# Stored split weights a step later, kept weight pieces two a step, and another order of PSUM pools in a two-layer trunk

## The chip, the cores and the metric

One core of a Trainium2 chip. The metric is the device time of one execution in microseconds (us), as the median of three runs. On the core work TensorE (PE in the profile; PEld is its weight load), VectorE (DVE), ScalarE (ACT), GpSimd (POOL) and SyncE (SP), which here only issues transfers (DMA).

## The reference

A trunk of two layers over 2048 frames of 1024 channels, all in float32:

```python
# layer A
h = rms_norm(x, a_norm);  u, z = split(h @ a_w_in)               # 1024 -> 2 x 1024
pooled = trailing_means(u, windows 2/4/8/16 by channel group) - u
x = x + ((grouped(pooled @ a_w_group) * a_scale) * silu(z)) @ a_w_out
x = x + (p[0] @ ple_w[0]) * sigmoid(x @ ple_gate_w[0])
# once, shared by layer B
k, v = split(rms_norm(x, kv_norm) @ w_kv);  k = rms_norm per head
# layer B
q, z = split(rms_norm(x, b_norm) @ b_w_in);  q = rms_norm per head
o = stick_breaking_attention(q, k, v)    # 16 heads of 64; A[t,s] = beta[t,s] * prod_{s<j<t}(1 - beta[t,j])
x = x + (o * silu(z)) @ b_w_out
x = x + (p[1] @ ple_w[1]) * sigmoid(x @ ple_gate_w[1])
```

## The kernel before

Every dense product is made of three TensorE passes. [...] A split takes one ScalarE instruction (copy, or a scaling by a norm's gain) and one subtract on VectorE or GpSimd. The split pair is twice as large as its source.

**First stage.** Four passes s = 0 to 3, one for each 512 frames. A pass has 22 steps (`STEPS`): 0 to 7 are `run_u` and `run_z` in turn for the four channel groups (some with a small group product, `run_m`), 8 to 11 `run_o` (output weights of layer A), 12 to 15 `run_g` (gate and per-layer embedding), 16 and 17 queries, 18 and 19 keys, 20 and 21 values (`run_kvq`). A step of 512 or 256 output channels has 48, 60 or 96 matmuls of 512 columns. The main loop (L541) first calls the load of the next step's weights (`load_w`), and then runs this step.

`load_w` (L94) loads units of 256 KB into `wraw` (3 buffers), splits each (L110 and L112, or with a gain L116 and L117) into `wpair` (12 buffers of 512 KB). The input weights of layer A (`wi`) are wanted in all four passes. In pass 0 each of their 32 split units is stored to DRAM (L121); passes 1 to 3 load them from there already split (L105).

Layer B's weights for z, output, gate and embedding are also split once, during the first stage, in 56 pieces (`keep`, L508): a raw load into pool `io` (L510), the split into a tile of tag `t4` (3 buffers; L178 and L179, or L517 and L518), a store to `wzd`, `wod`, `wgd` or `wld` (L520). The list `kept` is emptied by the main loop: in a pass before the last, one piece after each of the steps 8 to 21 and a second one after steps 8 and 12; in the last pass, one after each of the steps 8 to 15.

**Order of the work.** The kernel's text gives each instruction a place in program order. A scheduler in the compiler then makes each engine's own queue: it takes program order as the priority and fills in what it finds ready, by its own estimate of times. A buffer that is used again brings the waits with it. Some instructions are pinned behind their predecessor on the engine (`keep_in_program_order`). Once made, each engine's queue, SyncE's with the transfers included, runs strictly in its order.

**PSUM in the first stage.** Eight banks of 128 x 512: six for dense sums (`psd`), taken in turn, and two for transposes (`pst`). A value step (`token_major`, kind "v") reads its sums with ScalarE (L399), sends rows to the next partition by transfers issued from ScalarE (L403 to L410), and stores differences of values later (L416 to L420).

**Second stage.** Attention by 512 queries, heads and 512 keys. `front` makes logits (L607, L608, on the diagonal L610) in pool `psl`, then sigmoid (L613) and a running product (L615). `turn` transposes into `psa` (L626) and splits (L629, L630), `gather` sums values into `pso` (L638, L639). Between them, a generator `beside` gives pieces of dense work in `psd2`: `gate_z` for z (L667 to L671 in `piecewise`, weights loaded by L678 from `wzd`) and `post` for what comes behind attention. Four pools of two banks each are opened in the order `psl`, `psa`, `pso`, `psd2`, so they hold banks 0-1, 2-3, 4-5 and 6-7. A pool's first tile waits until the readers of what had stood in the pool's banks are done; SBUF pools of the second stage stand likewise on the first stage's.

Of the kernel before, what the change touches and what calls it, by code (L numbers as in the profile page):

```python
# [22 lines left out]
NSUB = S // W5  # L23
# [3 lines left out]
STEPS = 22  # L27
# [3 lines left out]
def f(ap):  # L31
    return ap.bitcast(F32)
# [3 lines left out]
def trunk_kernel(ctx, tc, x, p, a_norm, a_w_in, a_w_group, a_scale, a_w_out, kv_norm, w_kv,  # L36
                 k_norm, b_norm, b_w_in, b_q_norm, b_w_out, ple_w, ple_gate_w, out):
    nc = tc.nc
# [51 lines left out]

    state = {"w": 0, "first": True}
    split_once = {}

    def load_w(pools, src, kts, c0, n, gain=None, kept=None):  # L94


        wraw, wpair = pools
        units = []
        srcr = src.rearrange("(k q) n -> q k n", q=P)
        kk = min(W5 // n, kts)  # L100
        for k0 in range(0, kts, kk):
            pr = wpair.tile([P, 2, kk, n], F32R, tag="wpair", name="wpair")
            units.append(pr)
            if (kept, c0, k0) in split_once:
                nc.sync.dma_start(out=f(pr), in_=split_once[kept, c0, k0])  # L105
                continue
            raw = wraw.tile([P, kk, n], F32, tag="wraw", name="wraw")
            (nc.scalar if state["first"] else nc.sync).dma_start(out=raw, in_=srcr[:, k0 : k0 + kk, c0 : c0 + n])
            if gain is None:
                A.copy(out=pr[:, 0], in_=raw)  # L110
                state["w"] += 1
                (G if state["w"] % 3 else V).tensor_tensor(out=pr[:, 1], in0=raw, in1=f(pr[:, 0]), op=ALU.subtract)  # L112
            else:
                for j in range(kk):
                    g = gain[:, k0 + j : k0 + j + 1]
                    A.activation(out=pr[:, 0, j], in_=raw[:, j], func=AF.Identity, scale=g)  # L116
                    V.scalar_tensor_tensor(out=pr[:, 1, j], in0=raw[:, j], scalar=g, in1=f(pr[:, 0, j]),  # L117
                                           op0=ALU.mult, op1=ALU.subtract)
            if kept is not None:
                d = split_once[kept, c0, k0] = dram.tile([P, 2, kk, n], F32, name=f"{kept}_{c0}_{k0}")  # L120
                nc.sync.dma_start(out=d, in_=f(pr))  # L121
        return units

    def wst(units, kt, hl, c0, n=P):
# [19 lines left out]
    with ExitStack() as st:  # L144
# [32 lines left out]
        def split(pr, src, lo):  # L177
            A.copy(out=pr[:, 0], in_=src)  # L178
            lo.tensor_tensor(out=pr[:, 1], in0=src, in1=f(pr[:, 0]), op=ALU.subtract)  # L179
# [170 lines left out]
        def settle():  # L350
            while late:
                late.pop(0)()
# [108 lines left out]
        def turn_rows(dst, rows):  # L461
            n = rows.shape[0]
            pt = turned()
            T.transpose(pt[:, 0, :n], rows, ident[:n, :n])
            A.copy(out=dst, in_=pt[:, 0, :n])

        def load_gains(vs, dst):

            rows = t2.tile([len(vs) * KT, P], F32, tag="grow", name="grow", bufs=1)
            for i, v in enumerate(vs):  # L470
                nc.sync.dma_start(out=rows[i * KT : (i + 1) * KT], in_=v.rearrange("(k q) -> k q", q=P))
            turn_rows(dst, rows)

        def load_head_gains():
            rows = t2.tile([2, P], F32, tag="hrow", name="hrow", bufs=1)
            for i, v in enumerate((k_norm, b_q_norm[0])):
                for e in range(2):
                    nc.sync.dma_start(out=rows[i : i + 1, e * HD : (e + 1) * HD], in_=v.rearrange("(o d) -> o d", o=1))
            gs = t2.tile([P, 2], F32, tag="gs", name="gs", bufs=1)
            turn_rows(gs, rows)  # L480
            V.scalar_tensor_tensor(out=gqk, in0=gs[:, 1:2], scalar=HD ** -0.5, in1=gs[:, 0:1],
                                   op0=ALU.mult, op1=ALU.mult)

        steps = []
        for s in range(NSUB):
            for g in (3, 2, 1, 0):
                def load(g=g, z=0):
                    w = (load_w(wp, a_w_in[0], KT, z * D + g * 256, 256, g_a, "wi"),)
                    if z and g == 0:
                        w += (load_w(wp, a_w_group[0, 0], 2, 0, 256),)  # L490
                    if not z and g < 3:
                        w += (load_w(wp, a_w_group[0, g + 1], 2, 0, 256),)
                    return w
                steps.append((load, lambda *w, s=s, g=g: run_u(s, g, *w)))
                steps.append((lambda load=load: load(z=1), lambda *w, s=s, g=g: run_z(s, g, *w)))
            for b in range(4):
                steps.append((lambda b=b: (load_w(wp, a_w_out[0], KT, b * 256, 256),),
                              lambda *w, s=s, b=b: run_o(s, b, *w)))
            for b in range(4):
                steps.append((lambda b=b: (load_w(wp, ple_gate_w[0], KT, b * 256, 256),  # L500
                                           load_w(wp, ple_w[0], 2, b * 256, 256)),
                              lambda *w, s=s, b=b: run_g(s, b, *w)))
            for kind, wsrc, base, gain in (("q", b_w_in[0], 0, g_b), ("k", w_kv, 0, g_kv), ("v", w_kv, D, g_kv)):
                for b in range(2):
                    def load(wsrc=wsrc, base=base, b=b, gain=gain, s=s, kind=kind):
                        return (load_w(wp, wsrc, KT, base + b * W5, W5, gain),)
                    steps.append((load, lambda *w, s=s, kind=kind, b=b: run_kvq(s, kind, b, *w)))
        def keep(src, kts, k0, o, dst, gain=None):  # L508
            raw = io.tile([P, kts, P], F32, tag="io", name="kraw")
            nc.sync.dma_start(out=raw, in_=src.rearrange("(k q) n -> q k n", q=P)[:, k0 : k0 + kts, o * P : (o + 1) * P])  # L510
            pr = t2.tile([P, 2, kts, P], F32R, tag="t4", name="kpair", bufs=3)
            if gain is None:
                split(pr, raw, G)
            else:
                for j in range(kts):
                    g = gain[:, k0 + j : k0 + j + 1]
                    A.activation(out=pr[:, 0, j], in_=raw[:, j], func=AF.Identity, scale=g)  # L517
                    V.scalar_tensor_tensor(out=pr[:, 1, j], in0=raw[:, j], scalar=g, in1=f(pr[:, 0, j]),  # L518
                                           op0=ALU.mult, op1=ALU.subtract)
            nc.sync.dma_start(out=dst, in_=f(pr))  # L520

        kept = []
        for o in range(KT):
            for i in range(2):
                kept.append(lambda o=o, i=i: keep(b_w_in[0], 4, 4 * i, 8 + o, wzd[o][:, i], g_b))
                kept.append(lambda o=o, i=i: keep(b_w_out[0], 4, 4 * i, o, wod[o][:, i]))
                kept.append(lambda o=o, i=i: keep(ple_gate_w[1], 4, 4 * i, o, wgd[o][:, i]))
            kept.append(lambda o=o: keep(ple_w[1], 2, 0, o, wld[o]))
# [9 lines left out]
            pass  # L538
        load_gains([a_scale[0], b_norm[0], kv_norm], gains)
        load_head_gains()  # L540
        for i, (_, run) in enumerate(steps):  # L541
            after = steps[i + 1][0]() if i + 1 < len(steps) else None
            run(*ready)
            ready = after
            step, s = i % STEPS, i // STEPS
            if step >= 8 and (s + 1 < NSUB or step < 16):
                kept.pop(0)()
                if s + 1 < NSUB and step in (8, 12):
                    kept.pop(0)()
        assert not kept  # L550
        settle()


    with ExitStack() as st:
        wpair = st.enter_context(tc.tile_pool(name="wpair2", bufs=6))
        t2 = st.enter_context(tc.tile_pool(name="s2", bufs=2))
        kap = st.enter_context(tc.tile_pool(name="kap", bufs=1))
        psl = st.enter_context(tc.tile_pool(name="psl", bufs=2, space=bass.MemoryType.PSUM))
        psa = st.enter_context(tc.tile_pool(name="psa", bufs=2, space=bass.MemoryType.PSUM))
        pso = st.enter_context(tc.tile_pool(name="pso", bufs=2, space=bass.MemoryType.PSUM))  # L560
        psd = st.enter_context(tc.tile_pool(name="psd2", bufs=2, space=bass.MemoryType.PSUM))

        NK = 4
# [248 lines left out]
        for n in range(4 * len(slots) + LAG_G):  # L812
            i, j = divmod(n, 4)
# [60 lines left out]
```

## Time and profile before

| | us |
|---|---|
| median of 3 runs (lowest to highest) | 2873.58 (2870.37 to 2878.38) |
| the profiled execution's own time | 2875.26 |
| its span, first to last instruction | 2873.5 |
| TensorE busy | 2782.3 |
| VectorE busy | 1912.1 |
| ScalarE busy | 1404.5 |
| GpSimd busy | 859.3 |

The span leaves out what lies around the program's own instructions, 1.8 us here. The granted TensorE clock was 0.995 over the span. Busy time counts an engine as busy while an instruction of it runs; a matmul's end is modelled and matmuls overlap, so the time from one matmul's start to the next is what shows their pace. A row of waits names the waiting instruction, what released it, and total us, count and longest. A row of the timeline gives the start, the duration, engine, line, operation, the tiles written and read, the count of merged instructions, and in brackets the idle time before the first of them with what ended it. "SPq" and "ACTq" are the queues that issue transfers.

### The profile page before, as it was taken

What the parts mean: (1) busy time and instruction counts of PE and PEld (TensorE: products, weight loads), DVE (VectorE), ACT (ScalarE), POOL (GpSimd) and SP (SyncE); (2) the same over time, 40 slices, a digit from 0 to 9 for tenths busy, and PEclk for the clock granted to TensorE, in tenths of its full rate; (3) what the DMA queues carried; (4) which work ended last, traced back from release to release, by engine and by line L of the source; (5) the groups of instructions that cost most, each with busy time, mean ns of one, the idle gap of its engine ahead of it and who ended that gap; (6) DMA issues with size and microseconds to landing.
All of it is one profiled execution on the core that took longest, in us unless ns stands there. A gap on an engine that the chain in (4) does not pass through costs nothing. (4 is left out here: it accounts for less than half of the span.)

```text
span 2873.5 us, 40106 instructions
## 1 busy us (share of the span) xinstructions
PE 2782.3 (97%) x13923; PEld 2298.5 (80%) x13923; DVE 1912.1 (67%) x2584; ACT 1404.5 (49%) x2765; POOL 859.3 (30%) x710
## 2 busy tenths in 40 slices
PE   8899999999999999999899999999999999999999
PEld 6688788888888888888778888787878778878877
DVE  5645535455355544455399999999999998886642
ACT  4445523455234543345355555556566665564431
POOL 3474347543474425743211111110110011111110
PEclk9999999999999999999999999999999999999999
DMA  7746695457944688346657565555555565667764
GB/s 263 257 162 216 220 315 196 148 207 246 313 158 170 215 262 294 107 170 207 210 180 227 162 212 163 164 169 171 164 159 164 163 185 180 189 189 251 233 205 158
DMA packets 335133, 576.39 MB, mean 201 GB/s; under 512 B 32782, under 2 KB 161838, under 8 KB 334932
## 3 DMA queue, kind: packets, MB, share of 16 engines
q1 hardware_dynamic: 327944, 564.34, 59.7%
q10 hardware_dynamic: 6988, 9.50, 1.1%
q8 instruction: 110, 1.80, 0.3%
q14 instruction: 91, 0.75, 0.1%
HBM read 433.16 MB, written 132.19 MB: 197 GB/s over the span
## 5 line engine op out<-in xcount | busy, mean ns | idle before, releaser
L362 PE MATMUL psd<-wpair,x 128*128 128x512 f32 x2304 | 544.8, 393 | 0.0
L613 ACT ACTIVATE kap<-psl 128x512 f32<-128x512 f32 (+3 forms) x640 | 341.3, 534 | 411.7 <-PE psl L608 258.9
L615 DVE TENSOR_TENSOR_SCAN pp<-kap,pp,zeros 128x512 f32<-128x512 f32 x384 | 513.8, 1339 | 29.8 <-ACT kap L613 28.2
L362 PEld LDWEIGHTS psd<-wpair,x 128*128 128x128 f32 x2304 | 428.8, 188 | 86.4
L630 DVE TENSOR_TENSOR at<-psa,at 128x512 fp32r<-128x512 f32 (+3 forms) x640 | 373.9, 585 | 16.6 <-ACT at L629 15.7
L626 PE MATMUL psa<-ident,pp 128*128 128x128 f32 x2176 | 350.8, 276 | 32.4 <-DVE at L630 29.9
L629 ACT CAST at<-psa 128x512 fp32r<-128x512 f32 (+3 forms) x640 | 331.3, 518 | 38.4 <-PE psa L626 34.6
L626 PEld LDWEIGHTS psa<-ident,pp 128*128 128x128 f32 x2176 | 251.4, 141 | 111.2 <-DVE at L630 68.1
L615 DVE TENSOR_TENSOR_SCAN pp<-kap,zeros 128x128 f32<-128x128 f32 (+3 forms) x256 | 228.9, 894 | 70.4 <-ACT kap L613 68.7
L607 PE MATMUL psl<-kk,qa 128*128 128x512 f32 (+3 forms) x640 | 234.6, 367 | 4.6 <-ACT vr L399 4.6
L638 PE MATMUL pso<-at,vv 128*128 128x512 f32 (+3 forms) x640 | 235.3, 368 | 0.7 <-ACT at L629 0.6
L608 PE MATMUL psl<-kk,qb 128*128 128x512 f32 (+3 forms) x640 | 234.4, 366 | 0.0
L639 PE MATMUL pso<-at,vv 128*128 128x512 f32 (+3 forms) x640 | 233.6, 365 | 0.0
L133 PE MATMUL psd<-xp,wpair 128*128 128x512 f32 x512 | 201.3, 394 | 4.0 <-ACT xp L178 2.4
L135 PE MATMUL psd<-xp,wpair 128*128 128x512 f32 x512 | 201.4, 393 | 3.8 <-DVE wpair L117 3.7
L117 DVE SCALAR_TENSOR_TENSOR wpair<-wraw,gains,wpair 128x512 fp32r<-128x512 f32 x192 | 149.4, 790 | 83.3 <-ACT wpair L116 82.9
L134 PE MATMUL psd<-xp,wpair 128*128 128x512 f32 x512 | 200.9, 392 | 0.0
L116 ACT ACTIVATE wpair<-wraw,gains 128x512 fp32r<-128x512 f32 x192 | 136.7, 720 | 126.4 <-DMA wraw<-in_w_kv_dram 70.2
L711 POOL TENSOR_TENSOR zr<-zr,sgz 128x512 f32<-128x512 f32 x32 | 62.7, 1959 | 445.3 <-ACT sgz L710 288.2
L112 POOL TENSOR_TENSOR wpair<-wraw,wpair 128x512 fp32r<-128x512 f32 x107 | 146.9, 1381 | 78.7 <-ACT wpair L110 53.8
L110 ACT CAST wpair<-wraw 128x512 fp32r<-128x512 f32 x160 | 96.2, 619 | 126.4 <-DMA wraw<-in_a_w_out_dram 52.4
L607 PEld LDWEIGHTS psl<-kk,qa 128*128 128x128 f32 x640 | 120.8, 189 | 25.2 <-ACT vr L399 5.0
(209 smaller groups left out, 5593.5 us busy)
## 6 DMA issues: line engine op xcount, KB each, us to landing
wpair<-wi SPq DMA_DIRECT2D x96, 512.0 KB
kk<-kd SPq DMA_DIRECT2D x320, 128.0 KB
vv<-vd SPq DMA_DIRECT2D x160, 256.0 KB
wraw<-in_w_kv_dram SPq DMA_DIRECT2D x128, 256.0 KB
wpair<-wzd SPq DMA_DIRECT2D x64, 512.0 KB
wpair<-wod SPq DMA_DIRECT2D x64, 512.0 KB
wpair<-wgd SPq DMA_DIRECT2D x64, 512.0 KB
wi<-wpair SPq DMA_DIRECT2D x32, 512.0 KB
```

Of the source, the lines that this page charges most:

```text
L133: T.matmul(ps, wst(units, kt, 0, c0), acts[kt][:, 0], start=(kt == order[0]), stop=False)
L135: T.matmul(ps, wst(units, kt, 1, c0), acts[kt][:, 0], start=False, stop=(kt == order[-1]))
L362: T.matmul(pss2[i], ck["x2"][kt][:, xh, tk], wst(ws, kt, wh, 0, W5), start=(kt == 0 and xh == 0 and wh == 0), stop=(kt == KT - 1 and wh == 1))
L607: T.matmul(ps[:, :w], qa[:, qs], kk[:, :w], start=True, stop=False)
L608: T.matmul(ps[:, :w], qb[:, qs], kk[:, :w], start=False, stop=not st["diag"])
L613: A.activation(out=kp[:, r0:], in_=ps[:, :w], func=AF.Sigmoid, scale=-1.0)
L615: V.tensor_tensor_scan(out=pp[:, r0:][:, ::-1], data0=kp[:, r0:][:, ::-1], data1=zeros.to_broadcast([P, w]), initial=1.0 if st["diag"] els ...
L626: T.transpose(pt[:, j * P : (j + 1) * P], pp[:, r0 + kt * P : r0 + (kt + 1) * P], ident)
L629: A.copy(out=at[:, 0, cs], in_=pt[:, cs])
L630: V.tensor_tensor(out=at[:, 1, cs], in0=pt[:, cs], in1=f(at[:, 0, cs]), op=ALU.subtract)
L638: T.matmul(po[:, cs], vv[:, kt, :], at[:, 0, cs], start=(st["diag"] and kt == 0), stop=False)
L639: T.matmul(po[:, cs], vv[:, kt, :], at[:, 1, cs], start=False, stop=(st["last"] and kt == 3))
```

## The change

Three edits:

1. `load_w` no longer issues the store of a split unit. It puts it in a list; the main loop issues, after loading the next step's weights, the stores that were in the list before that load (`flush(behind)`). In program order a unit's store thus comes a step later, behind the next step's loads.
2. `keep` is cut in two. The raw load is issued after a step; the split and the store (`keep_pair`) follow in the next turn of the loop, after the weights' load and before that step's run. Pieces come only after steps 8 to 15 (beside the output and gate steps), two a step in passes 0 to 2 and one a step in pass 3.
3. The second stage's PSUM pools are opened in the order `pso`, `psa`, `psl`, `psd2`: value sums get banks 0 and 1, logits 4 and 5; the other two stay.

```diff
+    stores = []
+    def store(dst, src):
+        stores.append((dst, src))
+    def flush(n):
+        for _ in range(n):
+            dst, src = stores.pop(0)
+            nc.sync.dma_start(out=dst, in_=f(src))
...
                 d = split_once[kept, c0, k0] = dram.tile([P, 2, kk, n], F32, name=f"{kept}_{c0}_{k0}")
-                nc.sync.dma_start(out=d, in_=f(pr))
+                store(d, pr)
...
         def keep(src, kts, k0, o, dst, gain=None):
             raw = io.tile([P, kts, P], F32, tag="io", name="kraw")
             nc.sync.dma_start(out=raw, in_=src.rearrange("(k q) n -> q k n", q=P)[:, k0 : k0 + kts, o * P : (o + 1) * P])
+            return lambda: keep_pair(raw, kts, k0, dst, gain)
+
+        def keep_pair(raw, kts, k0, dst, gain):
             pr = t2.tile([P, 2, kts, P], F32R, tag="t4", name="kpair", bufs=3)
...
+        loaded = []
         for i, (_, run) in enumerate(steps):
+            behind = len(stores)
             after = steps[i + 1][0]() if i + 1 < len(steps) else None
+            flush(behind)
+            while loaded:
+                loaded.pop(0)()
             run(*ready)
             ready = after
-            step, s = i % STEPS, i // STEPS
-            if step >= 8 and (s + 1 < NSUB or step < 16):
-                kept.pop(0)()
-                if s + 1 < NSUB and step in (8, 12):
-                    kept.pop(0)()
-        assert not kept
+            if 8 <= i % STEPS < 16:
+                loaded = [kept.pop(0)() for _ in range(2 if i // STEPS + 1 < NSUB else 1)]
+        assert not kept and not stores
...
+        pso = st.enter_context(tc.tile_pool(name="pso", bufs=2, space=bass.MemoryType.PSUM))
+        psa = st.enter_context(tc.tile_pool(name="psa", bufs=2, space=bass.MemoryType.PSUM))
         psl = st.enter_context(tc.tile_pool(name="psl", bufs=2, space=bass.MemoryType.PSUM))
-        psa = st.enter_context(tc.tile_pool(name="psa", bufs=2, space=bass.MemoryType.PSUM))
-        pso = st.enter_context(tc.tile_pool(name="pso", bufs=2, space=bass.MemoryType.PSUM))
         psd = st.enter_context(tc.tile_pool(name="psd2", bufs=2, space=bass.MemoryType.PSUM))
```

## The prediction, made before the result was known

> **What bounds the kernel now.** I read the first part of the page, then who TensorE waited for.
>
> ```profile
> span 2873.5 us, 40106 instructions
> PE 2782.3 (97%) x13923; PEld 2298.5 (80%) x13923; DVE 1912.1 (67%) x2584; ACT 1404.5 (49%) x2765; POOL 859.3 (30%) x710
> ```
>
> TensorE has matmuls on it for 97% of the span, and the change removes none. All that it can win lies in the 2873.5 - 2782.3 = 91.2 us in which TensorE is idle, and in matmuls that run slower than they need.
>
> ```profile
> PE psa L626 <- DVE at L630: 29.9, 50, 1.6
> ...
> PE pst L445 <- DVE hl L454: 5.5, 3, 2.7
> ...
> PE psl L607 <- ACT vr L399: 4.6, 1, 4.6
> PE psd L667 <- DMA wpair<-wzd: 4.3, 1, 4.3
> ```
>
> Columns: total, times, longest, in us. The largest wait, 29.9 us on L630, is attention's own chain in the second stage. No line of it is edited; its banks move, its order in the loops does not. I give it 0 and come back to the banks. The wait of L445 belongs to the key and query steps, and the last two to the passage from the first stage to the second, one occurrence each.
>
> The rest of the idle time in the first stage is in its first pass. Here are the windows of five consecutive steps (4 to 8), cut where a step's first dense matmul starts, and one behind them (columns: TensorE busy and count, weight loads, DVE, ACT, POOL, granted clock, DMA share, GB/s):
>
> ```profile
> 67.80:86.50 18.70, 15.40 (x61) 11.68 (x60) 13.35 (x20) 7.05 (x16) 11.42 (x10) 0.91 0.62 208
> 86.50:98.70 12.20, 11.40 (x49) 8.83 (x49) 7.85 (x17) 4.92 (x12) 3.06 (x4) 1.00 0.93 330
> 98.70:113.50 14.80, 14.30 (x61) 11.03 (x60) 10.57 (x19) 6.19 (x13) 6.13 (x7) 1.00 0.80 265
> 113.50:132.80 19.30, 16.11 (x61) 12.17 (x60) 15.15 (x25) 9.48 (x21) 9.97 (x11) 0.91 0.81 280
> 132.80:149.10 16.30, 13.45 (x50) 9.99 (x49) 7.39 (x8) 6.75 (x12) 11.92 (x10) 0.90 0.58 194
> 149.10:182.50 33.40, 33.40 (x154) 27.75 (x152) 14.54 (x18) 13.30 (x23) 26.19 (x20) 1.00 0.48 157
> ```
>
> What these steps would take unhindered follows from the start times of matmuls in the timeline:
>
> ```profile
> 66.63 0.39 PE L134 MATMUL psd<-xp,wpair 128*128 128x512 f32 x1
> ...
> 72.07 0.39 PE L134 MATMUL psd<-xp,wpair 128*128 128x512 f32 x1
> 74.52 0.76 PE L135 MATMUL psd<-xp,wpair 128*128 128x512 f32 x1 [2.06 <-DVE wpair L117]
> ...
> 75.93 0.63 PE L135 MATMUL psd<-xp,wpair 128*128 128x512 f32 x1
> 76.36 0.63 PE L133 MATMUL psd<-xp,wpair 128*128 128x512 f32 x1
> ```
>
> From 66.63 to 72.07 lie 24 steps of 0.227 us; after the 2.06 us wait a matmul starts every 0.43 us (75.93 to 76.36), so the wait costs some 0.2 us more for each of the next five. At 0.227 us a matmul, a step of 48 is 10.9 us of work and one of 60 is 13.6. The five steps (60, 48, 60, 60, 48) are over it by 18.7 - 13.6 = 5.1, 12.2 - 10.9 = 1.3, 14.8 - 13.6 = 1.2, 19.3 - 13.6 = 5.7 and 16.3 - 10.9 = 5.4 us: **18.7 us in all**, the pool from which the first edit can draw.
>
> **Edit 1, stores of the split input weights behind the next loads.** No instruction is added or removed: 32 stores move. SyncE's queue, 15 to 133 us, shows what they do now, and ScalarE's waits, 20 to 150 us, what follows:
>
> ```profile
> SPq L121 <- DVE wpair L117: 50.3, 26, 5.0
> SPq L121 <- DVE t L253: 9.1, 3, 3.5
> ...
> ACT wpair L116 <- DMA wraw<-in_a_w_in_dram: 31.9, 11, 6.8
> ...
> 113.81 3.46 SPq L121 DMA_DIRECT2D wi<-wpair  x3
> 117.32 0.48 SPq L108 DMA_DIRECT2D wraw<-in_a_w_in_dram  x1
> ...
> 122.12 0.91 ACT L116 ACTIVATE wpair<-wraw,g_a 128x256 fp32r<-128x256 f32 x2 [5.71 <-DMA wraw<-in_a_w_in_dram]
> ```
>
> SyncE stands 59.4 us before stores whose split is not done; loads queue behind them. At 113.81 three stores (1.5 MB) go out ahead of the load at 117.32, whose data reach ScalarE at 122.12. At the window's 280 GB/s the 1.5 MB take 5.4 us of the DMA engines. With loads first, this one goes out up to 3.5 us sooner and has less ahead of it; TensorE's wait at the end of that chain is 0.8 us. By step: the second and third (1.3 + 1.2) wait for nothing but landed weights, and I take 2 of 2.5. In the fourth, the late split at 122.66 holds VectorE's pooling chain behind it, so a 2.0 us wait and slow matmuls follow; I take 4 of 5.7. In the fifth, the wait is for a subtract that stands in POOL behind kept pieces; I take 1 of 5.4. The first is no matter of loads, as VectorE's timeline shows:
>
> ```profile
> 68.08 1.79 DVE L179 TENSOR_TENSOR pp<-po,pp 128x512 fp32r<-128x512 f32 x1
> ...
> 74.39 0.68 DVE L179 TENSOR_TENSOR pp<-po,pp 128x512 fp32r<-128x512 f32 x1
> 74.99 3.21 DVE L518 SCALAR_TENSOR_TENSOR kpair<-kraw,gains,kpair 128x128 fp32r<-128x128 f32 x4
> 78.12 1.26 DVE L117 SCALAR_TENSOR_TENSOR wpair<-wraw,g_a,wpair 128x256 fp32r<-128x256 f32 x3
> ```
>
> VectorE runs without a gap there, and the L117 that TensorE awaits next stands at 78.12 behind 3.21 us of a kept piece. I take 0 of 5.1. Sum: **-7 us**, bounds 0 and -18.7. The stores lose nothing by coming later:
>
> ```profile
> L105 SPq DMA_DIRECT2D wpair<-wi x96: 319/390/1740, 357.5 to 1141.6; - x96
> L121 SPq DMA_DIRECT2D wi<-wpair x32: 319/338/362, 13.6 to 123.6; - x32
> ```
>
> The first read of wi is issued at 357.5 us, the last store at 123.6. A buffer of wpair is held until its store has landed, a step longer; twelve hold nearly three steps, so the fourth load of a step can come to wait for the store of two steps before. That store lands within its step, so I price it at 0.
>
> **Edit 2, kept pieces.** 56 pieces stay, each with a load of 256 KB (the eight of ple_w 128), a split on ACT and POOL or ACT and DVE, and a store of twice the size. In the text, 16 a pass come in steps 8 to 21 before; now 16 in steps 8 to 15, loaded a step ahead of the split. But where they run is another matter:
>
> ```profile
> L179 POOL TENSOR_TENSOR kpair<-kraw,kpair x40: 730/1292/1856, 43.4 to 1138.4; 128x512 fp32r<-128x512 f32 x32, 128x256 fp32r<-128x256 f32 x8
> ...
> L510 SPq DMA_DIRECT2D kraw<-in_b_w_in_dram x16: 368/432/963, 20.8 to 1117.9; - x16
> ...
> 142.94 0.50 SPq L510 DMA_DIRECT2D kraw<-in_ple_gate_w_dram  x1
> 255.52 0.43 SPq L510 DMA_DIRECT2D kraw<-in_b_w_in_dram  x1
> ```
>
> The first load is issued at 20.8 us, in step 0, though the text has it behind step 8: the text's order is a priority, and the queues are filled with whatever is ready. The tenth piece, the last of steps 8 to 15, loads at 142.94 us; the six of steps 16 to 21 follow from 255.52 on, with none between. So the split "two a step" will not be seen as such; six more pieces become available to the first pass, and the query and key steps lose six of theirs but can take the next pass's. Work on POOL: 6 x 4/7 x 1.29 = 4.4 us more before 237 us, where POOL is busy under 80% (26.19 of 33.40 us at 149.1 to 182.5). On the path: in the first key step a load stood in SyncE behind a kept store and L445 waited; its three waits are 5.5 us. The same pieces' successors can take that place. I take 0, bounds -5.5 and +10 (the rival below). SyncE's own waits on kept stores shrink, since a piece's data have landed a step before its split.
>
> **Edit 3, banks.** The last v step leaves its four sums in banks 4, 3, 2, 1 (six dense banks in turn). Logits had banks 0 and 1, so the first L607 waited for the very last L399; now value sums get 0 and 1, logits 4 and 5, whose readers are done.
>
> ```profile
> 1413.99 0.47 PE L607 MATMUL psl<-kk,qa 128*128 128x128 f32 x1 [4.61 <-ACT vr L399]
> ...
> 1416.00 0.31 PE L610 MATMUL psl<-maskr,identr 128*128 128x128 f32 x1
> 1420.61 0.77 PE L667 MATMUL psd<-x,wpair 128*128 128x512 f32 x1 [4.31 <-DMA wpair<-wzd]
> ...
> 1411.04 2.76 SPq L678 DMA_DIRECT2D wpair<-wzd  x2
> ...
> ACT kap L613 <- DMA vd<-vv: 4.5, 1, 4.5
> ...
> L613 ACT ACTIVATE kap<-psl x640: 271/597/659, 1429.7 to 2756.3; 128x512 f32<-128x512 f32 x96, 128x128 f32<-128x128 f32 x64
> ```
>
> The 4.6 us go, but behind them stand 2.3 us of matmuls and then the z weights, issued at 1411.04 and landed at 1420.6. Their transfer does not depend on banks. TensorE does its two fronts earlier and waits at the same place until the same moment; the third front needs ScalarE's first sigmoid, whose wait ends only with the landing of a vd store (1429.7, the first start of L613). What is late next is thus the wzd transfer, and the edit is worth 0; bounds -4.6 and +2.
>
> **Sum.** -7 + 0 + 0, against this execution's own 2875.26 us (span 2873.5 plus 1.8 around it): 2868.3. The median of the runs is 2873.58, 1.7 lower: 2866.6, said as **2867 us**.
>
> [...]
>
> **Rivals.** (a) *Nothing moves*, 2873 us, 17%: if the stores are placed where the order of readiness puts them, right behind their split, SyncE keeps standing at L121 and only the last places change; or the first pass is bound by the 3 MB a step, not by their order. For it: 330 GB/s and 0.93 share at 86.5 to 98.7 us. Against: 208 GB/s and 0.62 in the step with most idle time. [...]
>
> (b) *More goes*, 2856 us, 18%: with the order changed, kept pieces no longer fall in front of L117 and of POOL's subtracts in steps 4 and 8, and the whole 18.7 us go: 2873.6 - 18.7 = 2854.9; with one short wait left, 2856.
>
> (c) *Slower*, 2882 us, 14%: kept pieces land in the first pass's u and z steps, where VectorE is full. The first of the five steps shows the price: 5.1 us with kept pieces between. Six more, two to a step, are three such steps: +15.3, less the 7 of edit 1, +8.3: 2873.6 + 8.3 = 2882. It decides from about two such steps on (10.2 - 7 = +3). For it: pieces are taken as early as 20.8 us. Against: the loads of weights go first, and only ten got in by 143 us when ten were on offer.
>
> **How the numbers follow.** My forecast, -7 within -3 to -12, has 51%. What a measurement of this kernel can tell from no change I put at 0.3%, 8.6 us (the three runs spread over 8.0): faster means under 2865. Of the forecast's 51, 20 lie below that; with (b) 18 that is 0.38. Slower, over 2882.2: half of (c), a bad passage or a reshuffle of the second stage, 0.14. Same: the remaining 0.48. The range leaves out the far half of (b) and the far part of (c): 2856 to 2880.
>
> **What would show it.** Edit 1 right: SyncE's waits at the wi stores fall from 59 us to under 20, ScalarE's for in_a_w_in from 32 to under 20, and the window from the second to the fourth of these steps loses 6 us. Edit 2: first kraw load still far ahead of step 8, 16 loaded before the first query step, none of them in it. Edit 3: the first L607 no longer waits, and the first L667's wait grows to about 9 us. Wrong would be: a first L667 earlier than its 11 us behind the last L362, kept splits in front of L117 in more than two steps, or a different sum of L626's waits, 30 us now.

## The result: slower, and the profile after

| | before | after |
|---|---|---|
| median, us (lowest to highest) | 2871.97 (2869.92 to 2878.38) | 2906.74 (2904.20 to 2908.71) |
| end of the first stage in the profiled execution | 1409.4 | 1438.2 |
| from there to the end of the span | 1464.1 | 1464.1 |
| passes 0, 1, 2, 3 of the first stage | 369.4, 342.5, 343.7, 338.5 | 379.2, 353.1, 354.3, 336.7 |

The ratio is 1.0112, 95% interval 1.0100 to 1.0124; the forecast was 2867 with 2856 to 2880. The profiled executions differ by 28.9 us, all of it in the first stage, and only 9.8 of it in pass 0, the one pass that the prediction looked into. Steps are named by kind, pass and group: z1.0 is the last z step of pass 1. In the changed kernel lines stand lower: the dense product is L144 to L146 (high x high, high x low, low x high), its weights' load L119 and splits L121, L123, L127, L128; the late store is L102; `split` is L189 (a cast from f32 to fp32r, the high part) and L190 (a subtract of it from its source, the low part); a kept piece is loaded at L522, split at L532 and L533 (or L189 and L190), stored at L535; pooling runs from L250 to L265.

The first lines of the page after:

```profile
span 2902.4 us, 40122 instructions
PE 2789.1 (96%) x13923; PEld 2302.9 (79%) x13923; DVE 1915.2 (66%) x2584; ACT 1406.3 (48%) x2765; POOL 857.8 (30%) x710
```

The same matmuls, and TensorE's busy time grew by only 6.8 us; the rest is idle time. For whom it waited in the changed kernel (total, times, longest):

```profile
PE psa L643 <- DVE at L647: 29.9, 50, 1.6
PE psd L144 <- ACT pp L189: 15.3, 3, 8.1
PE psd L144 <- DVE ub L250: 6.0, 3, 2.9
...
PE psl L624 <- ACT vr L410: 5.4, 1, 5.4
...
PE psd L144 <- ACT x L189: 4.3, 1, 4.3
PE psd L144 <- ACT mp L189: 4.3, 2, 3.6
PE psd L684 <- DMA wpair<-wzd: 3.1, 1, 3.1
```

Attention's 29.9 us did not move. New are waits for `pp` and `ub`, the pooling chain between a u step and its group product. Windows of the changed kernel (TensorE, weight loads, DVE, ACT, POOL, clock, DMA share, GB/s): the five steps of pass 0 that were shown before, then g0.0, z1.0 and z2.0:

```profile
66.80:80.40 13.60, 13.60 (x61) 11.26 (x60) 11.31 (x20) 5.31 (x12) 6.31 (x7) 1.00 0.53 197
80.40:92.60 12.20, 11.15 (x49) 8.92 (x48) 7.34 (x11) 5.19 (x11) 2.92 (x3) 1.00 0.82 295
92.60:110.80 18.20, 15.60 (x62) 12.37 (x62) 14.39 (x23) 6.85 (x14) 8.31 (x9) 0.91 0.62 225
110.80:135.30 24.50, 15.79 (x61) 12.31 (x60) 14.30 (x23) 11.59 (x24) 15.06 (x16) 0.79 0.84 277
135.30:154.20 18.90, 13.71 (x49) 10.55 (x48) 10.78 (x13) 7.73 (x16) 13.76 (x12) 0.84 0.74 246
188.00:209.20 21.20, 16.54 (x64) 12.72 (x62) 7.80 (x11) 8.82 (x16) 14.09 (x11) 0.84 0.56 179
479.00:502.30 23.30, 16.70 (x62) 12.91 (x61) 13.30 (x17) 10.30 (x20) 15.68 (x15) 0.79 0.75 251
...
837.70:855.50 17.80, 15.73 (x61) 11.91 (x60) 14.54 (x16) 8.29 (x17) 15.23 (x14) 0.90 0.76 267
```

In the kernel before, z1.0 and z2.0 ran without a gap:

```profile
469.40:483.00 13.60, 13.60 (x62) 11.26 (x61) 9.43 (x12) 6.33 (x11) 9.95 (x11) 1.00 0.35 118
...
812.10:825.70 13.60, 13.60 (x61) 11.26 (x60) 12.06 (x12) 6.32 (x11) 13.28 (x12) 1.00 0.35 116
```

There VectorE began the pooling chain of z1.0 (L239, which is L250 after) 2.8 us into the step:

```profile
471.12 1.12 DVE L112 TENSOR_TENSOR wpair<-wraw,wpair 128x512 fp32r<-128x512 f32 x1 [4.60 <-ACT wpair L110]
472.16 1.28 DVE L239 TENSOR_TENSOR ub<-psd,rbx 128x512 f32<-128x512 f32 x2
```

The first of the five steps (u0.1) won 5.1 us; the next four lost 0.0, 3.4, 5.2 and 2.7; g0.0 lost 7.4, z1.0 9.7 and z2.0 4.3 (pass 2 lost another 3.1 in z2.1 and 2.5 in u2.0). Inside z1.0 three timelines of the changed kernel give the chain. ScalarE ("issue" means that nothing in the trace names what released it):

```profile
480.80 0.62 ACT L189 CAST kpair<-kraw 128x512 fp32r<-128x512 f32 x1 [4.49 <-issue]
...
486.13 1.28 ACT L532 ACTIVATE kpair<-kraw,gains 128x128 fp32r<-128x128 f32 x4 [1.61 <-DMA wzd<-kpair]
...
495.52 0.62 ACT L189 CAST pp<-po 128x512 fp32r<-128x512 f32 x1 [2.94 <-DVE po L260]
```

VectorE:

```profile
486.57 4.21 DVE L533 SCALAR_TENSOR_TENSOR kpair<-kraw,gains,kpair 128x128 fp32r<-128x128 f32 x4 [7.35 <-ACT kpair L532]
490.71 0.68 DVE L123 TENSOR_TENSOR wpair<-wraw,wpair 128x512 fp32r<-128x512 f32 x1
491.31 1.28 DVE L250 TENSOR_TENSOR ub<-psd,rbx 128x512 f32<-128x512 f32 x2
```

TensorE:

```profile
496.19 0.79 PE L144 MATMUL psd<-pp,wpair 128*128 128x512 f32 x1 [6.18 <-ACT pp L189]
...
498.43 0.63 PE L144 MATMUL psd<-pp,wpair 128*128 128x512 f32 x1
498.85 0.63 PE L145 MATMUL psd<-pp,wpair 128*128 128x512 f32 x1
```

Read from the end: the group product waits 6.18 us for `pp`, which needs the pooling chain that begins with L250 at 491.31. The sums it reads belong to u1.0, whose matmuls ended by 479.0. VectorE was not busy then: it stood idle for 7.35 us at L533, the lower half of a kept piece, whose upper half ScalarE made only at 486.13, after waits of its own at two kept pieces (4.49 and 1.61 us). L250 stood behind L533 in VectorE's queue and began 12.3 us into the step. Afterwards matmuls start every 0.42 us in place of 0.227.

### The profile page after: what moved, and what is told of

Its sections match the earlier page's. It is cut to its first block, busy times and chain, and to the rows that moved or that the text cites. A ratio compares the mean times of both kernels' runs of the same rounds, so it can differ in the third digit from the quotient of the medians.

```text
span 2902.4 us, 40122 instructions
## 1 busy us (share of the span) xinstructions
PE 2789.1 (96%) x13923; PEld 2302.9 (79%) x13923; DVE 1915.2 (66%) x2584; ACT 1406.3 (48%) x2765; POOL 857.8 (30%) x710
## 5 line engine op out<-in xcount | busy, mean ns | idle before, releaser
L630 ACT ACTIVATE kap<-psl 128x512 f32<-128x512 f32 (+3 forms) x640 | 341.3, 533 | 410.8 <-PE psl L625 259.3
L643 PE MATMUL psa<-ident,pp 128*128 128x128 f32 x2176 | 350.6, 276 | 32.9 <-DVE at L647 29.9
L144 PE MATMUL psd<-xp,wpair 128*128 128x512 f32 x512 | 202.2, 395 | 9.4 <-DVE ub L250 6.0
L128 DVE SCALAR_TENSOR_TENSOR wpair<-wraw,gains,wpair 128x512 fp32r<-128x512 f32 x192 | 150.2, 792 | 88.2 <-ACT wpair L127 87.7
L127 ACT ACTIVATE wpair<-wraw,gains 128x512 fp32r<-128x512 f32 x192 | 137.1, 720 | 140.5 <-DMA wraw<-in_w_kv_dram 88.9
L146 PE MATMUL psd<-xp,wpair 128*128 128x512 f32 x512 | 200.7, 392 | 0.0
L123 POOL TENSOR_TENSOR wpair<-wraw,wpair 128x512 fp32r<-128x512 f32 x107 | 145.4, 1364 | 81.7 <-ACT wpair L121 60.4
L121 ACT CAST wpair<-wraw 128x512 fp32r<-128x512 f32 x160 | 96.6, 618 | 118.7 <-PE psd L146 72.4
```

Of the source, the lines that this page charges most:

```text
L144: T.matmul(ps, wst(units, kt, 0, c0), acts[kt][:, 0], start=(kt == order[0]), stop=False)
L630: A.activation(out=kp[:, r0:], in_=ps[:, :w], func=AF.Sigmoid, scale=-1.0)
L643: T.transpose(pt[:, j * P : (j + 1) * P], pp[:, r0 + kt * P : r0 + (kt + 1) * P], ident)
```

## The experiments

Theory K: a kept piece's split stands, by the scheduler's order, in the queues of ScalarE and VectorE ahead of the pooling chain. Theory S: the late stores crowd the first pass. Ratios are against the kernel before, run beside each group (medians 2875.90, 2875.71, 2876.97 and 2874.33). Passes are read from each profiled execution.

| run | median | ratio [95%] | passes 0, 1, 2, 3 |
|---|---|---|---|
| 1 edit 1 alone | 2878.70 | 1.0012 [1.0002, 1.0021] | 372.6, 342.0, 347.1, 337.8 |
| 2 edit 2 alone | 2902.31 | 1.0093 [1.0077, 1.0110] | 373.5, 353.9, 356.1, 336.7 |
| 3 edit 3 alone | 2874.93 | 1.0001 [0.9992, 1.0011] | 368.8, 342.0, 344.6, 338.4 |
| 4 change, splits held | 2868.96 | 0.9979 [0.9969, 0.9988] | 364.5, 343.7, 343.6, 336.7 |
| 5 old spread, loaded ahead | 2894.10 | 1.0066 [1.0051, 1.0081] | 376.5, 349.4, 346.9, 338.4 |
| 6 two a step, not ahead | 2899.43 | 1.0082 [1.0065, 1.0100] | 378.6, 350.1, 352.0, 336.8 |
| 7 run 4 without edit 1 | 2874.25 | 0.9995 [0.9986, 1.0005] | 369.3, 343.6, 342.4, 336.7 |
| 8 four buffers | 2907.95 | 1.0106 [1.0091, 1.0122] | 384.3, 352.6, 352.9, 341.3 |
| 9 before, splits held | 2887.28 | 1.0042 [1.0026, 1.0059] | 373.5, 343.4, 350.3, 342.1 |
| 10 run 4, loads held too | 2906.92 | 1.0106 [1.0092, 1.0120] | 379.7, 355.4, 355.4, 338.9 |
| 11 run 4, pass 0 a step later | 2871.12 | 0.9985 [0.9976, 0.9994] | 364.0, 344.0, 343.0, 336.7 |
| 13 run 4, not ahead | 2892.17 | 1.0057 [1.0040, 1.0073] | 376.7, 348.5, 347.7, 339.1 |
| 14 run 4, all four held | 2872.41 | 0.9994 [0.9985, 1.0002] | 364.9, 343.4, 343.9, 336.7 |
| 15 run 14 without edit 1 | 2873.06 | 0.9993 [0.9984, 1.0002] | 367.2, 342.8, 342.7, 336.7 |
| 16 run 14, pass 0 a step later | 2866.29 | 0.9973 [0.9962, 0.9984] | 361.7, 343.2, 342.8, 336.7 |
| 17 only gained pieces held | 2886.31 | 1.0042 [1.0028, 1.0055] | 372.3, 350.1, 348.8, 336.7 |

**Runs 1 to 3: one edit each.** Each is the kernel before with one edit of the change.

> The kernel before with the first edit alone (stores of split input weights behind the next loads). Theory K (the loss comes from kept pieces: their splits now stand in the queues of ScalarE and VectorE in front of the pooling chain of the last u step, and wait there): this kernel has none of it and keeps the gain in pass 0, about 2872 - 6 = 2866 us, with no TensorE wait on pp of more than 2 us. Theory S (the late stores crowd pass 0 and shift all that follows): 2885 us or more, with most of the loss before 240 us.

> The kernel before with the second edit alone (kept pieces two a step in steps 8 to 15, loaded a step ahead of the split). Theory K: the +10 us of pass 1 and of pass 2 return, and some of pass 0: 2872 + 20 to 35 = 2892 to 2907 us, with TensorE waits on pp of 5 us or more in the last z step of a pass. Theory S: within 5 us of before, 2867 to 2877.

> The kernel before with the third edit alone (order of the PSUM pools). Both theories: within 3 us of before, 2869 to 2875 us; the first logits matmul starts right behind the last value matmul, and the first z matmul waits some 4 us longer.

Edit 2 carries the loss, with the whole change's pattern: z1.0 takes 23.2 us, g0.0 21.8. Edit 3 is nothing. Run 1 is a miss for the numbers of both theories: no 7 us were won, TensorE waits 7.8 us for `pp`, and 2885 is not reached. It does win u0.1 (13.6), but z0.0 takes 24.7 in place of 19.3. Five kept splits run in it, three in the kernel before, so even edit 1, which touches no kept piece, moved them; a second cause shows at runs 14 and 15.

**Run 4: hold the splits.** Edit on the whole change:

```diff
-                split(pr, raw, G)
+                tc.keep_in_program_order(A.copy(out=pr[:, 0], in_=raw))
+                G.tensor_tensor(out=pr[:, 1], in0=raw, in1=f(pr[:, 0]), op=ALU.subtract)
...
+                    if j == 0:
+                        tc.keep_in_program_order(ins)
```

> The changed kernel with the first split instruction of each kept piece (ScalarE's) pinned behind what the text has before it on that engine, so that the pieces really fall into the output and gate steps. Theory K: the waits of the z steps go, and the time is under that of before, 2860 to 2870 us. Theory S: it stays at 2890 us or more, since the stores are those of the changed kernel.

K is borne out: nothing but the place of ScalarE's part is fixed, and some 38 us go (1.0112 to 0.9979). Loads and stores of the pieces move along, and the DMA share in z1.0 falls from 0.75 to 0.32; but a busy DMA alone did not lengthen a z step in the kernel before: z2.1 (787.6 to 798.5 us) ran in 10.9 us without a gap at a share of 0.91. The windows of z1.0 and z2.0 in run 4:

```profile
464.30:477.90 13.60, 13.60 (x61) 11.26 (x60) 7.36 (x11) 6.25 (x11) 8.66 (x9) 1.00 0.32 98
808.00:821.60 13.60, 13.60 (x61) 11.26 (x60) 7.39 (x10) 6.35 (x11) 10.77 (x9) 1.00 0.31 96
```

**Runs 5, 6: which half of edit 2?** Run 5 has `step >= 8` and the counts of the kernel before, on `loaded`; run 6 has `kept.pop(0)()()` two a step.

> The whole change, but the kept pieces keep the places they had before (steps 8 to 21 of a pass, one a step, two in steps 8 and 12); only the new load a step ahead of the split stays. Theory K (a kept split that stands in the in-order queues of ScalarE and VectorE ahead of the pooling chain costs the step; where it stands decides): in the instruction order of this kernel no kept split stands in the last z step of passes 1 and 2, where the change lost 9.7 and 4.3 us, but seven stand in the last u and z step of pass 0. So passes 1 and 2 go back to 342 to 346 us each and pass 0 stays near 379: 2875.9 + 10 = 2880 to 2888. Rival L (the load ahead is the harm, wherever the splits stand): passes 1 and 2 stay at 353, 2900 or more. Rival T (two a step is the harm): all comes back, 2870 to 2877.

> The whole change, with two pieces in each of steps 8 to 15, but load and split of a piece stand together again, as before. Theory K: in the instruction order no kept split stands in the last z step of passes 1 and 2 here either (they stand in the u and z steps ahead of it, up to four to a u step), and seven in the last u and z step of pass 0. Pass 0 near 379, passes 1 and 2 at 342 to 348: 2880 to 2890. Rival L (the load ahead is the harm): 2870 to 2877. Rival T (two a step is the harm): passes 1 and 2 at 353, 2898 to 2906.

Both numbers missed: the order in which the built program lists its instructions did not tell in which step a split would run. Counted in the trace, the splits that started inside a step go with its length. In z1.0: none 13.6 (before, runs 4, 7, 9), one 18.9 (run 5), three 21.0 to 23.3 (after, runs 2, 6, 8). In z2.0: none 13.6, one 13.6 (run 5), three 17.8 and 17.9, four 21.4 and 21.6. So neither half is innocent. Runs 5 and 6 both contain edits 1 and 3; with these, the load ahead costs 0.66%, two a step 0.82%, and the two together 1.12%: they overlap, since each pushes splits into the same steps.

**Runs 7, 9: holding without parts of the change.** Run 7 is run 4 with the store back at its old place; run 9 holds the splits in the kernel before.

> The fourth experiment (the whole change with the first ScalarE instruction of each kept split held at its place in the program's order) with the stores of the split input weights back where they were before, so without the first edit. It tells what the first edit is worth once kept pieces are out of the way of the early u and z steps. If later stores win what the prediction said, 7 us, then this is 2874 to 2878 against the fourth experiment's 2869.0. If they win nothing, as the first experiment has it: 2867 to 2871. If they cost (that experiment: +2.8): 2864 to 2867.

> The kernel before, none of the three edits, with the first ScalarE instruction of each kept split held at its place. It tells whether the holding alone, without the change, makes the fourth experiment's gain. Theory K: kept splits leave the u and z steps of all passes; before lost in them some 5 us in the first of the five steps and little in passes 1 to 3, and the query, key and value steps keep their pieces and the waits at L445: 2868 to 2874. If two pieces a step in the output and gate steps are worth something once they stay there: this one is 2 us or more above the fourth experiment's 2869.0.

Run 7 lands where a gain of 7 us for edit 1 would have it: 2874.25 us, 5.3 more than run 4. But the five steps that the gain was forecast for show none: from u0.1 to o0.0 run 4 takes 76.9 us and run 7 75.9. The difference is q0.0 (24.2 us in run 4, 29.8 in run 7) and g0.0 (13.7 and 15.6); what lengthens a query step is in the last section.

Run 9 is a clear miss: holding alone costs 0.42%. Its u and z steps of passes 1 and 2 are clean, but q0.0 takes 31.4 us (before: 22.7), q2.0 30.2 and q3.0 28.1. ScalarE's waits in q0.0 of run 9:

```profile
ACT wpair L116 <- DMA wraw<-in_b_w_in_dram: 5.6, 2, 4.8
...
ACT kpair L518 <- DMA kraw<-in_b_w_in_dram: 2.9, 1, 2.9
```

A kept split that is held, but whose load goes out right in front of it, makes ScalarE stand 2.9 us, with query weights behind it. It is not the whole cause: in q3.0 ScalarE waits at no kept split.

**Runs 8, 10, 11, 13.** Run 8: `bufs=4` for tag `t4`, `bufs=7` for `tmp`. Run 10: the raw load wrapped in `keep_in_program_order`. Run 11: `first = 9 if i < STEPS else 8`, pieces in steps `first` to `first + 7`. Run 13: run 4 with `kept.pop(0)()()`.

> The whole change with four instead of three buffers for the split pair of a kept piece (and the tiles that share its tag); the room comes from one of the eight buffers of tag tmp. Theory K1: in the last z step of passes 1 and 2 it is ScalarE that stands still at a kept split because all three pair buffers still wait for their stores to land (6 us of ScalarE's waits in that step, the split at L189 and at L532), and the pooling chain behind it comes late. With a fourth buffer that wait goes down, and the step's loss of 9.7 (pass 1) and 4.3 us (pass 2) at least halves: 2885 to 2898. Theory K2: it is the work itself, the kept splits' own microseconds on ScalarE and VectorE ahead of the chain, buffers or not: both steps stay within 2 us of what they were, 2902 to 2910. The buffer taken from tmp can cost some us in the key and query steps by either theory; these are read apart from the z steps.

> The fourth experiment (first ScalarE instruction of each kept split held at its place), with the loads of kept pieces held at their places too. In the fourth experiment eight of these loads went out in the last z step of pass 0, ahead of weights, and ScalarE waited 3.9 us for one of them with the pooling chain behind it; that step took 21.6 us against 15.2 in the seventh. If these loads are what crowds it: z0.0 at 15 to 17, in all 2862 to 2866. If the one kept split that still stands there (or the stores of the split input weights) is what counts: z0.0 at 20 or more, 2867 to 2871.

> The fourth experiment with the kept pieces of pass 0 one step later (steps 9 to 16 in the place of 8 to 15), the other passes as they were. In its instruction order no kept split stands in the last z step of pass 0, one stands in the u step ahead of it. Theory K: that z step goes from 21.6 to about 15 to 17 us and the query step, which gets two pieces, loses 1 to 2: 2862 to 2867, the fastest version so far. If the late stores of the input weights are what makes the step long, it stays: 2868 to 2872.

> The fourth experiment with load and split of a kept piece together again in the text (two a step, steps 8 to 15, held): tells what the load a step ahead is worth once the splits stay in place. The ninth experiment, also held and without the load ahead, had ScalarE wait 2.9 and 3.2 us in query steps at a kept split for its own load, and was 11.6 us slower than before. If the load ahead is what spares that: 2874 to 2882. If the late steps (16 to 21) were the ninth's trouble and not the missing load ahead: 2867 to 2871.

Run 8 clears the buffers: z1.0 takes 23.0 us and z2.0 21.4 (that one 3.5 us longer than in the changed kernel, with four kept splits in place of three, where theory K2 said within 2), and its VectorE shows the same picture in z1.0 with ScalarE's wait for a store gone (ScalarE still stood 5.1 us at kept L189, released by nothing that the trace names):

```profile
491.29 5.04 DVE L533 SCALAR_TENSOR_TENSOR kpair<-kraw,gains,kpair 128x128 fp32r<-128x128 f32 x4 [6.25 <-ACT kpair L532]
496.25 0.68 DVE L123 TENSOR_TENSOR wpair<-wraw,wpair 128x512 fp32r<-128x512 f32 x1
496.85 1.27 DVE L250 TENSOR_TENSOR ub<-psd,rbx 128x512 f32<-128x512 f32 x2
```

Run 13 says what the load ahead is worth once splits are held: 1.0057 against 0.9979, some 22 us, in q0.0 (36.5 us), q1.0 (29.7) and q2.0 (29.1); that is more than either forecast. Run 10 missed both of its ranges by some 40 us: held loads go out late, q1.0 takes 36.5 us, and z0.0 still 22.6. Run 11 missed K's number: with the pieces a step later z0.0 still takes 24.0 us, and the time lies in the range given for late stores.

**Runs 14 to 17: what was still open.** In runs 4 and 11 only the first of four ScalarE instructions was held, and the other three with their VectorE halves (three quarters of a split) still ran in z0.0 ahead of L250. Run 14 holds all four (`tc.keep_in_program_order(A.activation(...))` for each `j`), run 15 is that without edit 1, run 16 that with pass 0 a step later, run 17 the whole change with only the 16 pieces with a gain held.

> The fourth experiment with all four ScalarE instructions of a split with a gain held in place, not the first alone; in its instruction order no kept split stands ahead of the first output step of any pass. Theory K: the last u and z step of pass 0 go from 17.6 and 21.6 us to about 15 each: 2869 less 7 to 9, 2859 to 2864, the fastest version. Theory S (the late stores crowd that step): both stay, 2866 to 2872.

> The same with the stores of the split input weights where they were before (no first edit). Against the run before it, this is what the first edit is worth with no kept split in the way. If the prediction's -7 holds there: 5 to 9 us slower than that run. If late stores win nothing, as the first experiment has it: within 3 us of it. Under theory S it is 5 us or more faster.

> All held, and the pieces of pass 0 one step later (steps 9 to 16). With no kept split in the last z step in either version, the later place wins nothing there and gives two pieces to a query step: 0 to 3 us slower than the version with steps 8 to 15. If the loads of kept pieces (they go out two steps ahead) are what crowds the last z step, it is 3 us or more faster.

> The whole change with the ScalarE instructions of the 16 pieces with a gain held (their lower half is VectorE's work), the 40 without a gain (ScalarE and POOL) free. If it is VectorE's queue alone that costs (kept splits with a gain ahead of the pooling chain): 2862 to 2876. If ScalarE's queue counts as much (pieces without a gain too, waiting for a load or a buffer ahead of the pooling chain's own split): the u and z steps stay long, 2890 or more.

Runs 14 and 15 differ by 0.65 us of median: with no kept split in the way, edit 1 is worth nothing that these medians show. They get there by different ways. z0.0 of run 14, then of run 15:

```profile
109.70:130.00 20.30, 15.66 (x61) 12.32 (x60) 11.69 (x19) 8.37 (x15) 11.96 (x13) 0.92 0.96 293
```

```profile
110.70:125.90 15.20, 14.17 (x62) 10.92 (x60) 10.76 (x19) 6.75 (x13) 6.74 (x8) 1.00 0.71 235
```

With late stores no kept load goes out before z0.0, and then eight do in it; the DMA share is 0.96. The next step's weights land late, and their split holds up the same chain, as VectorE's timeline of run 14 shows:

```profile
118.12 0.69 DVE L123 TENSOR_TENSOR wpair<-wraw,wpair 128x512 fp32r<-128x512 f32 x1 [6.82 <-ACT wpair L121]
118.73 1.28 DVE L250 TENSOR_TENSOR ub<-psd,rbx 128x512 f32<-128x512 f32 x2
```

Without edit 1, z0.0 is 5.2 us shorter, o0.0 6.7 longer (17.5 against 10.9). K's forecast for run 14 (2859 to 2864) fell with this: no kept split stands in z0.0, and it still takes 20.4 us. S is right as to this one step. The kept loads are not what holds the chain up: in run 10, at a DMA share of 0.60, VectorE waits just as long at L123, and the first kept load of that step goes out only at 121.80 us:

```profile
120.66 0.69 DVE L123 TENSOR_TENSOR wpair<-wraw,wpair 128x512 fp32r<-128x512 f32 x1 [6.46 <-ACT wpair L121]
121.27 1.28 DVE L250 TENSOR_TENSOR ub<-psd,rbx 128x512 f32<-128x512 f32 x2
```

What all versions with edit 1 share is that the loads of the next weights (output weights) begin 2.7 to 4.4 us ahead of z0.0, and the split of one of them stands in front of the chain; without edit 1 these loads begin 3.7 to 5.4 us into the step. In the twelve traces with edit 1 L250 starts 8.6 to 13.6 us into z0.0, in the six without it 1.9 to 3.3. It is K's mechanism again, with a split that belongs to the next step.

Run 16 has the lowest time, 0.27% (0.16 to 0.38%) under the kernel before; run 4's interval (0.12 to 0.31%) overlaps it. Its profile differs from run 14's mostly in q0.0 (24.1 against 27.8 us). It is 6.1 us faster than run 14, as the second half of its forecast allowed, but not for the reason given there: z0.0 still has its eight kept loads and takes 20.2 us. Run 17 sits between the two theories' numbers: its u and z steps of passes 1 and 2 are clean (98.4 us a pass, as in run 4), although eight kept splits still run in them in pass 1, six without a gain and two with one. None of them is in u1.0 or z1.0. So a split of either kind did no harm in the earlier steps, and which kind does it in z1.0 is not told apart: the place is what changed. It loses in g0.0 (17.5) and in the query steps (29.8, 31.2, 29.7). In a query step the count of kept splits does not decide: two started in q2.0 of run 4 (23.8 us), one in q1.0 of run 17 (31.2).

## Why the prediction was wrong, point by point

**The step that failed is edit 2's term: 0, bounds -5.5 and +10.** Alone it costs 0.93%, 26.4 us by the medians. The runs show in its place kept splits whose data or buffers come late, in front of the pooling chain in the queues of ScalarE and VectorE: 9.7 us in z1.0 alone, all of it gone when the splits are held (run 4). The 0 weighed the pieces' work against the room for it ("where POOL is busy under 80%"). VectorE had room too, 7.35 us of idle time in z1.0, and just this idle time was the harm: what cost was the place in the queue ahead of L250, which began 12.3 us into the step in place of 2.8, not the work. The upper bound came from the price of one kind of step in pass 0; passes 1 and 2 were not looked at, because the trace of before shows no idle time in their u and z steps. Yet before held 10 kept splits in steps z1.3 to u1.0, none in z1.0. Edit 2 moved six a pass out of the query, key and value steps and so lengthened that train by one step, into z1.0. There the chain has the least slack: group 0's product follows its u step after one z product, while for the other groups a z and a further u product lie between.

What the prediction expected to see of edit 2 was in part there: 16 kept loads before the first query step and none in it, and the hoped-for end of the wait in the first key step (k0.0 29.0 to 25.3 us). But the first load, said to stay far ahead of step 8, went from 20.8 us to 113.8, into step 7. The loads of kept pieces in the first 300 us after:

```profile
L522 SPq DMA_DIRECT2D kraw<-in_b_w_in_dram x6: 413/527/1333, 113.8 to 296.0; - x6
L522 SPq DMA_DIRECT2D kraw<-in_b_w_out_dram x5: 462/468/490, 116.5 to 173.5; - x5
...
```

**Rival (c) named the mechanism, but for one pass and too cheaply.** It put kept splits into u and z steps at 5.1 us a step, three steps, pass 0 alone. The traces show up to 9.7 us a step, and passes 1 and 2 with 10.5 and 10.6 each, more than pass 0 (9.8).

**Edit 1: -7 forecast, +0.12% alone, -5.3 us in the pair 4 and 7 by way of a query step, nothing in the pair 14 and 15.** The waits of SyncE (15 to 133 us) and ScalarE (20 to 150 us) after:

```profile
SPq L119 <- DVE wpair L128: 52.5, 28, 7.3
...
```

```profile
ACT wpair L127 <- DMA wraw<-in_a_w_in_dram: 25.2, 13, 4.5
```

The forecast was under 20 for both. SyncE's waits at the stores are gone, as forecast, and stand now at the loads: a load needs a raw buffer, that is held until VectorE's split (L128), and only three exist. The prediction took the queue's standing still for a matter of order; the split's pace sets it. By step, gains of 0, 2, 4 and 1 us were forecast for the first, the second and third, the fourth and the fifth step; measured in the whole change were 5.1, -3.4, -5.2 and -2.7. The 5.1 is rival (b)'s: no kept split runs in u0.1 any more. The fourth step, z0.0, was to gain most and became longer in every version with edit 1 (20.2 to 26.1 us, without it 14.9 to 19.3): loads that go out sooner brought their split in front of the chain. No run shows a source for the -3 at the near end of the forecast's range; what they show is +0.12% alone, -5.3 us in the first pair and nothing in the second.

**Edit 3: 0 forecast, 0 measured, by another way.** The first logits matmul was to wait no longer; it waits 5.4 us after and 5.2 in run 3 (before 4.6), for the same line (L410 after, L399 before). TensorE's timeline after:

```profile
1443.62 0.47 PE L624 MATMUL psl<-kk,qa 128*128 128x128 f32 x1 [5.37 <-ACT vr L410]
...
1449.07 0.76 PE L684 MATMUL psd<-x,wpair 128*128 128x512 f32 x1 [3.15 <-DMA wpair<-wzd]
```

So the inference on which banks these readers hold was wrong, or the wait is not the bank's; no trace names a bank, and no run tells these apart. That the z weights' landing ends the passage either way held.

**The length of a kept split on VectorE.** Four instructions of L533 took 4.21 us at 486.57, while POOL was busy for some 3.8 of them, and 1.23 in z0.0 at 119.58, while POOL stood idle (5.13 us, to 122.45). The 3.0 us between them are a part of the 9.7 lost in z1.0, not its size. No run tells whether it is POOL's work that lengthened the one.

## What to carry to other kernels

When a scheduler hoists background work, ask in which engine's queue it will stand, in front of whom, and when its own data come; a step with idle engines can still be the worst place (z1.0: VectorE idle for 7.35 us, 9.7 us lost). Price every repetition of such a place, also where the trace of before shows no idle time (passes 1 and 2: 10.5 and 10.6 us). The same goes for the next step's own weights when their loads are moved forward (z0.0: 20.3 us in run 14, 15.2 in run 15). Holding background work where it is written paid here only together with loads that are early enough (ratio 0.9979 in run 4, 1.0057 in run 13); holding every ScalarE instruction of a piece in place of the first won nothing more (0.9994 in run 14).

## What was not expected of the hardware

A wait of TensorE cost more here than the wait. In q1.0 of run 17 TensorE waits once for 2.41 us, and the step is 8.5 us longer than in the changed kernel (31.2 against 22.7). The start of the slow stretch and its windows in run 17 (the clock is the column before the DMA share):

```profile
597.43 0.50 PE L373 MATMUL psd<-wpair,x 128*128 128x512 f32 x1 [2.41 <-ACT x L189]
```

```profile
590.00:598.00 8.00, 5.30 (x21) 3.35 (x19) 4.08 (x7) 3.51 (x6) 3.81 (x3) 0.99 0.79 304
598.00:606.00 8.00, 7.84 (x22) 6.52 (x23) 0.94 (x3) 2.35 (x5) 2.55 (x4) 0.50 0.71 243
606.00:616.00 10.00, 10.00 (x41) 8.16 (x40) 5.91 (x9) 4.46 (x7) 4.81 (x4) 0.90 0.33 105
```

From 598 to 606 us the granted clock is 0.50 while TensorE is busy: 14 matmuls of 512 columns and eight of one column run, where at 0.227 us each 35 of 512 columns would fit. The length of the wait did not set that of the slow stretch. In the clock's record it lasts 10.2 us here and in z1.0 of the changed kernel, whose wait was 6.18 us; in q0.0 a wait of 2.31 to 2.32 us was followed by 3.4 us of it in run 14 (step 27.8 us), 6.8 in run 17 (29.8) and 10.2 in run 9 (31.4). What sets it stays open. In these traces it goes with the long query steps: every first query step over 27 us has a wait of TensorE of 1.46 us or more and 3.4 to 17.1 us at 0.50 with it; where the waits stay under 1 us (run 4: 22.7 to 24.2) the clock stays at 1.00.
